# Banded attention with score tiles of 64 queries of two heads instead of 128 queries of one head

## The chip, the cores and the metric

The kernel runs on one core of a Trainium2 chip. The metric is the device time of one execution in microseconds (us). Three executions of the kernel before took 2079.76, 2080.51 and 2081.54 us, so the median is 2080.51 us. Five engines work side by side and meet through semaphores: PE (TensorE, matrix products into the PSUM banks), DVE (VectorE), ACT (ScalarE), POOL (GpSimd) and SP (it issues most of the transfers). PEld is the loading of PE's stationary operand.

## The reference

One encoder layer is applied to two sequences that share their weights, a sample of 1024 tokens and a prompt of 512, all in float32. Normalised tokens go through one input projection (2048 to 5632); half of the mix is a gated convolution branch, the other half is attention in a window; both are multiplied by a gate, joined, projected by `w_out`, added to the input and normalised. The part around the change is this:

```python
def banded_sink_attention(q, k, v, sink):        # 8 query heads, 2 key heads (GROUP = 4), head size 128
    ...                                          # query block b of 128 sees key blocks b-1, b, b+1
    s = jnp.einsum("bnqkgd,bnjkd->bnkgqj", qb, kb).astype(jnp.float32) * scale
    rel = kpos[:, None, :] - qpos[:, :, None]
    valid = (jnp.abs(rel) <= WINDOW) & (kpos[:, None, :] >= 0) & (kpos[:, None, :] < S)   # WINDOW = 128
    s = jnp.where(valid[None, :, None, None], s, -1e30)
    m = jnp.maximum(jnp.max(s, axis=-1, keepdims=True), sink_f)
    p = jnp.exp(s - m)
    denom = jnp.sum(p, axis=-1, keepdims=True) + jnp.exp(sink_f - m)
    probs = (p / denom).astype(v.dtype)
    o = jnp.einsum("bnkgqj,bnjkd->bnqkgd", probs, vb)
```

A query sees at most 257 keys: those at a distance of up to 128. All scores that are computed beyond that get the value -1e30 and come out of the exponential as zero.

## The kernel before

**Products.** Each float32 operand is split into a high part (rounded to the type float32r, by ACT) and a low part (the rest, by DVE); `parts` (L506) does this. A product is then three matmuls into one PSUM bank: high by high, high by low, low by high. The projections run as a written-out list of work items: `Unit` and `Onto` (L94, L271) multiply 2 by 2 blocks by Strassen's scheme with seven products, each of 12 matmuls with 512 columns (L207), and `Job` (L386) is a plain product of 512 columns (L670). PE works through this list for nearly the whole run.

**Lanes.** All else (convolution taps, normalisation, attention) is written as Python generators that sit in three lanes (`Lane`, L64). After every three matmuls of the list, `tick` gives each lane credit in ns, and a lane takes steps while it has credit; a `yield S1` says what the step is held to cost. So attention's matmuls are put between the matmuls of the projections. A scheduler then orders the instructions of each engine by priority (`high_priority`) and by when their operands come free.

**Attention.** `group` (L1116) holds keys and values of one key head and goes through the blocks of 128 queries: 8 blocks by 2 groups for the sample, in the trace from 876 to 1290 us, while the prompt's projections run on PE; 4 blocks by 2 groups for the prompt, from 1391 to 1670 us, while the sample's convolution output and then its output projection run. `attention` (L1151) does one block for the four heads of a group:

- the queries are split (L1160), and those of the next block are loaded (L1149, from `q_d` in device memory, where `rotated` and `rotate` stored them, L1073 to L1079);
- for each head, three matmuls (L1168) make a tile `s` of 128 queries by 384 keys (256 in the first and last block of a sequence); there are two PSUM buffers `s`;
- one DVE instruction (L1171) scales the tile, adds the mask, and writes it to a tile `p` together with the maximum of each row. `p` tiles come from a set of four buffers (`PT`, L487), which other parts of the program use too;
- ACT takes the exponential (L1182), with the row sums, and multiplies by the reciprocal (L1189);
- for each block of 128 keys, PE turns the four tiles (L1202, matmuls against the identity) into one PSUM tile `pt`, ACT and DVE split it into `a`, and three matmuls of 512 columns (L1197) add to `pv`;
- ACT copies `pv` out (L1210) and SP stores it in `att_d`.

**POOL** does nothing in the sample's attention. While the prompt's second group is under way, it issues the transfers of `Onto.begin` (L285): each loads a tile that a later product is added to, into a buffer `g` or `u`, and waits until that buffer's last user is done. Instructions of one engine run in order, so what stands behind such a transfer waits as well.

Of the kernel before, what the change touches and what calls it, by code (L numbers as in the profile page):

```python
# [25 lines left out]
LN_EPS = 1e-5  # L26
SCALE = P ** -0.5


# [401 lines left out]
class Encoder:  # L431
# [129 lines left out]
    def constants(self):  # L561
# [15 lines left out]
        def rest():  # L577
            self.ident = load("ident", [P])
            self.mask = load("mask", [3 * P])
# [166 lines left out]
class Sequence:  # L746


    def __init__(self, e, s):
# [322 lines left out]

    def rotated(self, dst, accs):  # L1073
        self.e.store(dst, self.rope(accs[0], 0))

    def rotate(self, dst):
        def done(t, z):
            self.e.store(dst[:, t * W : t * W + W], self.rope(z, t, z))
            yield  # L1079

        return done
# [26 lines left out]
    def query(self, h, accs):  # L1108
        self.rotated(self.q_d[h // GROUP][:, h % GROUP], accs)
        self.asked(h)  # L1110
# [35 lines left out]
    def load_query(self, g, b, room=None):  # L1146
        if b < self.B:
            self.q = room or self.e.U([GROUP, P])
            self.e.nc.sync.dma_start(self.q, self.q_d[g][:, :, b * P : (b + 1) * P])  # L1149

    def attention(self, g, b, k, v):  # L1151

        e, nc, B = self.e, self.e.nc, self.B
        lo, hi = max(b - 1, 0), min(b + 2, B)
        n = (hi - lo) * P
        keys = slice(lo * P, hi * P)
        mask = e.mask[:, (lo - b + 1) * P : (hi - b + 1) * P]
        qs = e.A([2, GROUP, P])
# [5 lines left out]
        pr = []  # L1164
        for h in range(GROUP):
            ps = e.PS("s", [3 * P])
            for p, (x, y) in enumerate(((0, 0), (0, 1), (1, 0))):
                nc.tensor.matmul(ps[:, 0:n], qs[:, x, h], k[y][:, keys], start=p == 0, stop=p == 2)  # L1168
            p = e.PT("p", NP, [W])
            with e.tc.high_priority(SOON):  # L1170
                nc.vector.tensor_tensor_reduce(  # L1171
                    p[:, 0:n], ps[:, 0:n], mask, SCALE, e.sink[:, g * GROUP + h : g * GROUP + h + 1],
                    ALU.add, ALU.max, accum_out=m[:, h : h + 1],
                )
            pr.append(p)
            if h % 2:
                yield S6
        with e.tc.high_priority(SOON):
            nc.vector.tensor_scalar(nm, m, -1.0, None, ALU.mult)  # L1179
            nc.vector.tensor_tensor(es, e.sink[:, g * GROUP : (g + 1) * GROUP], m, ALU.subtract)  # L1180
            for h, p in enumerate(pr):
                nc.scalar.activation(p[:, 0:n], p[:, 0:n], AF.Exp, bias=nm[:, h : h + 1], accum_out=l[:, h : h + 1])  # L1182
            nc.scalar.activation(es, es, AF.Exp)
        yield S2
        with e.tc.high_priority(SOON):
            nc.vector.tensor_tensor(l, l, es, ALU.add)
            nc.vector.reciprocal(r, l)
            for h, p in enumerate(pr):
                nc.scalar.activation(p[:, 0:n], p[:, 0:n], AF.Identity, scale=r[:, h : h + 1])  # L1189
        yield S4  # L1190
# [8 lines left out]
        for i in range(hi - lo):  # L1199
            tp = e.PS("pt", [GROUP, P])  # L1200
            for h, p in enumerate(pr):
                nc.tensor.transpose(tp[:, h], p[:, i * P : (i + 1) * P], e.ident)  # L1202
# [12 lines left out]
    def units(self):  # L1215
# [19 lines left out]
        rest = gates[:2] + [  # L1235
            both((K + g, V + g), f"kv{g}", each(self.rotate(self.k_d[g]), self.value_of(g))) for g in range(2)
        ]
        for h in range(HEADS):
            turn = self.rotate(self.q_d[h // GROUP][:, h % GROUP])
            rest.append(both((Q + h, AG + h), f"q{h}", each(turn, self.silu_of(self.ag_d[h]))))  # L1240
        return conv, rest + gates[2:]

    def jobs(self):
# [7 lines left out]
        kv = lambda g: [  # L1251
            job(K + g, lambda acc: self.rotated(self.k_d[g], acc)),
            job(V + g, lambda acc: self.value(g, acc)),
# [923 lines left out]
```

## Time and profile before

| what | value |
|---|---|
| median of three executions | 2080.51 us |
| span of the profiled execution, first to last instruction | 2072.4 us |
| profiled execution's own time | the page lists the span alone; the median lies 8.1 us above it |
| PE busy | 2057.6 us, 99% of the span |
| DVE busy | 1752.3 us, 85% |
| ACT busy | 1043.9 us, 50% |
| POOL busy | 157.8 us, 8% |
| DMA engines, share of 16 | q1 (SP) 61.6%, q0 (POOL) 12.1% |

"Busy" of PE counts from the start of a matmul to a modelled end, so 99% does not say how fast PE is within that time; the distance from one start to the next in the timeline does. The lines by group give the count and mean length of each kind of instruction; the list of waits says what an engine stood idle for.

### The profile page before, as it was taken

How to read it: one execution, taken by the hardware profiler on the slowest of the kernel's cores; microseconds unless marked ns; L12 is line 12 of the kernel's file. 1: busy time of each engine (PE TensorE's matmuls, PEld its weight loads, DVE VectorE, ACT ScalarE, POOL GpSimd, SP SyncE). 2: the span in 40 equal slices, each digit the busy share in tenths (PEclk: the TensorE clock that was granted, in tenths of full speed). 3: DMA queues.
4: the chain of work that ended last, by engine and by line, in shares of the span. 5: the costliest groups of instructions: out<-in, count | busy, mean ns of one | idle time of the engine just before them, and what ended most of it. 6: DMA issues, size and time to landing. Idle time of an engine off the chain costs nothing.

```text
span 2072.4 us, 27195 instructions
## 1 busy us (share of the span) xinstructions
PE 2057.6 (99%) x9256; PEld 1696.0 (82%) x9256; DVE 1752.3 (85%) x2873; ACT 1043.9 (50%) x1711; POOL 157.8 (8%) x240
## 2 busy tenths in 40 slices
PE   9999999999999999999999999999999999999998
PEld 8888888888888888788888888888888888888886
DVE  8767899998899999889866877767799978998877
ACT  7485445333464443644455777336454343454454
POOL 0111111101111112100000000000000111100000
PEclk9999999999999999999999999999999999999999
DMA  8888786864577776954455555997789899678897
GB/s 295 312 299 254 197 222 220 292 214 154 193 242 192 178 173 172 290 169 154 159 172 187 176 183 182 317 331 235 246 288 302 281 317 297 206 249 297 290 334 275
DMA packets 242300, 494.56 MB, mean 239 GB/s; under 512 B 23664, under 2 KB 84464, under 8 KB 242160
## 3 DMA queue, kind: packets, MB, share of 16 engines
q1 hardware_dynamic: 216352, 428.83, 61.6%
q0 software_dynamic: 24512, 61.88, 12.1%
q10 hardware_dynamic: 1296, 2.11, 0.3%
q8 instruction: 72, 1.18, 0.2%
q14 instruction: 68, 0.56, 0.1%
HBM read 331.77 MB, written 160.96 MB: 238 GB/s over the span
## 4 chain that ended last, share of the span: by engine, by line
PE 52%; issue 7%; DVE 4%; DMA 2%; POOL 1%; ACT 1%; POOLq 0%; ACTq 0%; SPq 0%; DVEq 0%
PE a L670 14%; PE c L670 7%; PE b L670 7%; PE a L207 7%; PE c L207 3%; PE s L1168 2%; PE pv L1197 2%; PE s L1851 2%; PE a L1851 2%; PE b L207 1%; PE pt L1202 1%; DVE hl L511 1%; PE pt L1851 1%; PE pv L1851 1%; POOL u L501 1%
## 5 line engine op out<-in xcount | busy, mean ns | idle before, releaser
L207 PE MATMUL a<-t,hl 128*128 128x512 f32 x2640 | 633.1, 390 | 2.0 <-ACT g L236 1.3
L207 PEld LDWEIGHTS a<-t,hl 128*128 128x128 f32 x2640 | 493.2, 188 | 109.5 <-ACT g L236 2.6
L510 ACT ACTIVATE hl<-raw 128x1024 fp32r<-128x1024 f32 (+3 forms) x334 | 296.1, 890 | 375.3 <-PE c L207 90.6
L511 DVE TENSOR_TENSOR hl<-raw,hl 128x1024 fp32r<-128x1024 f32 (+3 forms) x334 | 337.9, 1012 | 143.6 <-ACT hl L510 142.0
L670 PE MATMUL a<-t,hl 128*128 128x512 f32 x1344 | 325.8, 393 | 0.0
L207 PE MATMUL c<-t,hl 128*128 128x512 f32 x1320 | 319.2, 389 | 0.0
L670 PEld LDWEIGHTS a<-t,hl 128*128 128x128 f32 x1344 | 248.9, 188 | 50.2
L207 PEld LDWEIGHTS c<-t,hl 128*128 128x128 f32 x1320 | 247.4, 188 | 51.5 <-DVE u L304 0.2
L1041 DVE SCALAR_TENSOR_TENSOR f<-f,c_w_dw,f 128x512 f32<-128x512 f32 x248 | 173.3, 745 | 0.3
L670 PE MATMUL b<-t,hl 128*128 128x512 f32 x672 | 163.6, 393 | 1.3 <-DVE t L515 0.8
L1004 DVE SCALAR_TENSOR_TENSOR f<-f,c_w_dw,f 128x512 f32<-128x512 f32 x232 | 163.7, 745 | 1.0 <-ACT f L999 0.9
L670 PE MATMUL c<-t,hl 128*128 128x512 f32 x672 | 164.4, 393 | 0.0
L207 PE MATMUL b<-t,hl 128*128 128x512 f32 x660 | 159.8, 389 | 0.0
L670 PEld LDWEIGHTS b<-t,hl 128*128 128x128 f32 x672 | 124.6, 188 | 27.4 <-DVE t L515 1.1
L670 PEld LDWEIGHTS c<-t,hl 128*128 128x128 f32 x672 | 124.7, 188 | 24.7
L207 PEld LDWEIGHTS b<-t,hl 128*128 128x128 f32 x660 | 123.7, 188 | 25.6
L1033 DVE SCALAR_TENSOR_TENSOR f<-f,w_both,f 128x512 f32<-128x512 f32 x120 | 89.8, 748 | 2.3 <-ACT f L1027 0.3
L236 ACT ACTIVATE u<-a 128x512 f32<-128x512 f32 x82 | 48.7, 594 | 69.7 <-PE a L207 66.9
L236 ACT ACTIVATE g<-a 128x512 f32<-128x512 f32 x78 | 46.4, 595 | 70.0 <-PE a L207 65.1
L1182 ACT ACTIVATE p<-p,tiny 128x384 f32<-128x384 f32 (+1 forms) x96 | 54.5, 570 | 44.1 <-DVE tiny L1179 25.2
L510 ACT ACTIVATE a<-pt 128x512 fp32r<-128x512 f32 x64 | 38.0, 593 | 63.9 <-PE pt L1202 63.6
L418 ACT ACTIVATE hl<-raw 128x1024 fp32r<-128x1024 f32 x43 | 45.4, 1056 | 47.1 <-PE a L670 18.7
(354 smaller groups left out, 2713.0 us busy)
## 6 DMA issues: line engine op xcount, KB each, us to landing
raw<-w_in SPq DMA_DIRECT2D x170, 512.0 KB, 5.2
raw<-w_out SPq DMA_DIRECT2D x31, 512.0 KB, 5.3
raw<-w_pw SPq DMA_DIRECT2D x24, 512.0 KB, 4.2
wsum_P<-raw SPq DMA_DIRECT2D x47, 256.0 KB, 3.5
raw<-wsum_P SPq DMA_DIRECT2D x18, 512.0 KB, 4.7
f<-x_s SPq DMA_DIRECT2D x16, 512.0 KB, 8.7
g<-wsum_P SPq DMA_DIRECT2D x28, 256.0 KB, 4.4
a<-sum_S SPq DMA_DIRECT2D x24, 256.0 KB, 6.7
```

What stands on the lines that cost most here:

```text
L207: nc.tensor.matmul(acc, hl[:, l, o, j, :], toks[j][:, r], start=name in FRESH and j == 0 and q == 0, stop=name in LAST and j == HALF - 1 a ...
L236: nc.scalar.activation(t, bank, AF.Copy)
L418: e.nc.scalar.activation(t[:, 0], raw, AF.Copy)
L510: nc.scalar.activation(hi, x, AF.Copy)
L511: nc.vector.tensor_tensor(lo, x, hi.bitcast(F32), ALU.subtract)
L670: nc.tensor.matmul(job.acc[0], hl[:, l, kk // HALF, kk % HALF, :], r, start=i == 0 and p == 0, stop=i == nk - 1 and p == 2,)
L1004: nc.vector.scalar_tensor_tensor(t, h[:, j : j + T], w(j), t, ALU.mult, ALU.add)
L1033: nc.vector.scalar_tensor_tensor(m0, odd[:, j : j + H], both(j), m0, ALU.mult, ALU.add)
L1041: nc.vector.scalar_tensor_tensor(out, d[:, j : j + H], w(2 * j + k), out if j else m0, ALU.mult, ALU.add)
L1168: nc.tensor.matmul(ps[:, 0:n], qs[:, x, h], k[y][:, keys], start=p == 0, stop=p == 2)
L1182: nc.scalar.activation(p[:, 0:n], p[:, 0:n], AF.Exp, bias=nm[:, h : h + 1], accum_out=l[:, h : h + 1])
L1851: nc.tensor.matmul(acc[t], self.toks[name, m][:, x, i, t * P : (t + 1) * P], parts[i][l].rearrange("p a b -> p (a b)"), start=fresh and fi ...
```

## The change

A score tile now holds 64 queries of two heads: the first 64 rows are one head, the others the next head with the same 64 positions. Such a tile needs the keys from 128 before its first query to 128 after its last, 320 in place of 384; at the ends of a sequence 192 for the outer half and 256 for the inner. A block still has four tiles (two pairs of heads by two halves), with three matmuls each. The queries lie in device memory so that one load brings them in this order; to store them takes pieces of 64 values in place of 512. Mask and sinks are laid out to fit. The columns of `p` that no score is written to (64 of them in each tile that has fewer columns than its block has keys) are set to zero by GpSimd, since the turning of the tiles still takes blocks of 128 keys. Its output now goes to two heads by 64 queries of `pt`.

```diff
@@ Sequence
-        self.q_d = dram("q_d", [GROUP, self.T], 2)
+        self.q_d = dram("q_d", [GROUP // 2, self.T // HQ, 2, HQ], 2)
...
+    def rows_of_query(self, h):
+        pair, odd = divmod(h % GROUP, 2)
+        dst = self.q_d[h // GROUP][:, pair, :, odd, :]
+        n = W // HQ
+        return lambda t, z: self.e.store(dst[:, t * n : t * n + n], z.rearrange("p (n q) -> p n q", q=HQ))
...
     def load_query(self, g, b, room=None):
         if b < self.B:
             self.q = room or self.e.U([GROUP, P])
-            self.e.nc.sync.dma_start(self.q, self.q_d[g][:, :, b * P : (b + 1) * P])
+            src = self.q_d[g][:, :, 2 * b : 2 * b + 2].rearrange("p c a h q -> p c (a h q)")
+            self.e.nc.sync.dma_start(self.q.rearrange("p (c a) x -> p c (a x)", c=GROUP // 2), src)
 
     def attention(self, g, b, k, v):
...
-        n = (hi - lo) * P
-        keys = slice(lo * P, hi * P)
-        mask = e.mask[:, (lo - b + 1) * P : (hi - b + 1) * P]
+        tiles = []
+        for pair in range(GROUP // 2):
+            for half in range(2):
+                at = b * P + half * HQ
+                k0, k1 = max(at - P, 0), min(at + HQ + P, self.T)
+                tiles.append((slice(2 * pair, 2 * pair + 2), slice(half * HQ, half * HQ + HQ), k0, k1, k0 - at + P))
...
-        for h in range(GROUP):
+        for h, (heads, qr, k0, k1, at) in enumerate(tiles):
+            n = k1 - k0
             ps = e.PS("s", [3 * P])
             for p, (x, y) in enumerate(((0, 0), (0, 1), (1, 0))):
-                nc.tensor.matmul(ps[:, 0:n], qs[:, x, h], k[y][:, keys], start=p == 0, stop=p == 2)
+                nc.tensor.matmul(ps[:, 0:n], qs[:, x, h], k[y][:, k0:k1], start=p == 0, stop=p == 2)
             p = e.PT("p", NP, [W])
+            left, right = k0 - lo * P, hi * P - k1
+            if left:
+                nc.gpsimd.memset(p[:, 0:left], 0.0)
+            if right:
+                nc.gpsimd.memset(p[:, left + n : left + n + right], 0.0)
+            valid = p[:, left : left + n]
             with e.tc.high_priority(SOON):
                 nc.vector.tensor_tensor_reduce(
-                    p[:, 0:n], ps[:, 0:n], mask, SCALE, e.sink[:, g * GROUP + h : g * GROUP + h + 1],
+                    valid, ps[:, 0:n], e.mask[:, at : at + n], SCALE, e.sink[:, g * GROUP + h : g * GROUP + h + 1],
                     ALU.add, ALU.max, accum_out=m[:, h : h + 1],
                 )
...
-            for h, p in enumerate(pr):
-                nc.tensor.transpose(tp[:, h], p[:, i * P : (i + 1) * P], e.ident)
+            for (p, _), (heads, qr, *_) in zip(pr, tiles):
+                nc.tensor.matmul(
+                    tp[:, heads, qr], p[:, i * P : (i + 1) * P], e.ident.rearrange("p (h q) -> p h q", q=HQ),
+                    start=True, stop=True, is_transpose=True,
+                )
```

The exponential (L1182) and the multiplication (L1189) now work on `valid` as well. The order of the instructions shows three places.

On PE, in the sample's second block (the first with neighbours on both sides); `s` are score tiles, `t` the keys' parts, `a` the queries' parts, the others are the prompt's projections. Before:

```order
L1168 MATMUL s_7902<-t_966_7575,a_7866 128x384
L1168 MATMUL s_7902<-t_967_7576,a_7866 128x384
L1168 MATMUL s_7902<-t_966_7575,a_7866 128x384
L1168 MATMUL s_7908<-t_966_7575,a_7866 128x384
L1168 MATMUL s_7908<-t_967_7576,a_7866 128x384
L1168 MATMUL s_7908<-t_966_7575,a_7866 128x384
L670 MATMUL a_7879<-t_935_7399,hl_7810 128x512 x3
```

And now:

```order
L1183 MATMUL s_7904<-t_966_7575,a_7868 128x320
L1183 MATMUL s_7904<-t_967_7576,a_7868 128x320
L1183 MATMUL s_7904<-t_966_7575,a_7868 128x320
L1183 MATMUL s_7911<-t_966_7575,a_7868 128x320
L1183 MATMUL s_7911<-t_967_7576,a_7868 128x320
L1183 MATMUL s_7911<-t_966_7575,a_7868 128x320
L671 MATMUL a_7881<-t_935_7399,hl_7812 128x512 x3
```

The matmuls stand at the same place and are as many; each has 64 columns fewer.

On PE, the first turning of the same block's four tiles, with what each waits for. Before:

```order
L1202 MATMUL pt_8015<-c_ident,p_7906 128x128 [waits Activation_49]
L1202 MATMUL pt_8015<-c_ident,p_7912 128x128 [waits Activation_49]
L1202 MATMUL pt_8015<-c_ident,p_7924 128x128 [waits Activation_49]
L1202 MATMUL pt_8015<-c_ident,p_7930 128x128 [waits Activation_49]
```

And now:

```order
L1223 MATMUL pt_8021<-c_ident,p_7908 128x2x64 [waits Activation_49]
L1223 MATMUL pt_8021<-c_ident,p_7915 128x2x64 [waits Activation_49,Pool_49]
L1223 MATMUL pt_8021<-c_ident,p_7928 128x2x64 [waits Activation_49]
L1223 MATMUL pt_8021<-c_ident,p_7935 128x2x64 [waits Activation_49,Pool_49]
```

Tiles whose zeros stand in this block of keys make their matmul wait for POOL too. In the whole program, 20 of these matmuls waited for two engines before, and 64 do now.

On POOL and DVE, in the prompt's last block of the second group. POOL before:

```order
L285 DMA u_14576<-xT_s 128x512
L285 DMA g_14465<-xT_s 128x512
L285 DMA g_14549<-xT_s 128x512
L285 DMA g_14637<-xT_s 128x512
```

POOL now (`p_14498` and `p_14539` are the second and the fourth tile of the block):

```order
L286 DMA u_14656<-xT_s 128x512 [waits DMAHW3_49,DMAHW0_49,DMASW2_49]
L286 DMA g_14545<-xT_s 128x512 [waits DMAHW2_49,DMASW3_49]
L1187 MEMSET p_14498 128x64 [waits PE_49,Pool_49]
L286 DMA g_14629<-xT_s 128x512 [waits DMAHW3_49,DMAHW7_49,DMASW4_49,DVE_49]
L1187 MEMSET p_14539 128x64 [waits PE_49,Pool_49]
L286 DMA g_14717<-xT_s 128x512 [waits DMAHW0_49,DMASW5_49,DVE_49]
```

DVE now, around the fourth tile (`hl` are weights in two parts, `f` a convolution, L305 adds a finished product to its tile):

```order
L1192 ISA p_14539,tiny_14461<-s_14535,c_mask,c_attn_sink 128x192 [waits PE_49,Pool_49]
L1192 ISA tiny_14461 128x1
L1007 TENSOR_TENSOR f_13809<-f_13809 128x512 [waits DVE_49]
L1200 TENSOR_SCALAR tiny_14462<-tiny_14461 128x4 [waits DVE_49]
L1201 TENSOR_TENSOR tiny_14463<-c_attn_sink,tiny_14461 128x4
L305 TENSOR_TENSOR g_14449<-a_14339,g_14449 128x512 [waits DMAHW6_49,DMASW7_49,PE_49]
L512 TENSOR_TENSOR hl_14578<-raw_14376,hl_14578 128x1024 [waits Activation_49]
L305 TENSOR_TENSOR u_14475<-a_14547,u_14475 128x512 [waits DMAHW6_49,DMASW0_49,PE_49]
```

There are 80 memsets in all: 64 in the 16 blocks with neighbours on both sides, 16 in the 8 blocks at an end. 75 of the 96 DVE instructions of the score tiles wait for POOL, because the memset is the first to write the buffer and the others find out through it that the buffer is free; before, none did.

More of the change, by code (lines that the diff above doesn't have):

```diff
@@ L27 @@
 SCALE = P ** -0.5
+HQ = P // 2
 VAL, GLU, GATE, Q, K, V, AG = 0, 8, 16, 24, 32, 34, 36
@@ L1108, in query @@
     def query(self, h, accs):
-        self.rotated(self.q_d[h // GROUP][:, h % GROUP], accs)
+        self.rotated(self.rows_of_query(h), accs)
         self.asked(h)
@@ L1187, in attention @@
             nc.vector.reciprocal(r, l)
-            for h, p in enumerate(pr):
-                nc.scalar.activation(p[:, 0:n], p[:, 0:n], AF.Identity, scale=r[:, h : h + 1])
+            for h, (_, p) in enumerate(pr):
+                nc.scalar.activation(p, p, AF.Identity, scale=r[:, h : h + 1])
         yield S4
@@ L1235, in units @@
         rest = gates[:2] + [
-            both((K + g, V + g), f"kv{g}", each(self.rotate(self.k_d[g]), self.value_of(g))) for g in range(2)
+            both((K + g, V + g), f"kv{g}", each(self.rotate(self.rows_of(self.k_d[g])), self.value_of(g))) for g in range(2)
         ]
         for h in range(HEADS):
-            turn = self.rotate(self.q_d[h // GROUP][:, h % GROUP])
+            turn = self.rotate(self.rows_of_query(h))
             rest.append(both((Q + h, AG + h), f"q{h}", each(turn, self.silu_of(self.ag_d[h]))))
@@ L2154 @@
         arrays[name] = g[name].reshape(-1, P).T
-    arrays["attn_sink"] = np.broadcast_to(g["attn_sink"][0][None], (P, HEADS))
+    sink = g["attn_sink"][0].reshape(HEADS // 2, 2)[:, None, :, None]
+    arrays["attn_sink"] = np.broadcast_to(sink, (HEADS // 2, 2, 2, HQ)).transpose(2, 3, 0, 1).reshape(P, HEADS)
     half = P // 2
@@ L2162 @@
     arrays["sin"] = np.concatenate([sin, -sin])
-    q, k = np.arange(P)[:, None], np.arange(3 * P)[None] - P
+    q, k = np.arange(P)[:, None] % HQ, np.arange(2 * P + HQ)[None] - P
     arrays["mask"] = np.where(np.abs(k - q) <= P, f(0), f(-1e30)).astype(f)
```

20 lines of the change are left out of this document (11 added, 9 removed).

## The prediction

> **What bounds the kernel now.** I read the page's busy times first, then the windows of the two stretches with attention, then what PE waited for.
>
> ```profile
> span 2072.4 us, 27195 instructions
> PE 2057.6 (99%) x9256; PEld 1696.0 (82%) x9256; DVE 1752.3 (85%) x2873; ACT 1043.9 (50%) x1711; POOL 157.8 (8%) x240
> ```
>
> ```profile
> core 0: us, PE busy (x) PEld busy (x) DVE busy (x) ACT busy (x) POOL busy (x), PEclk, DMA share, GB/s
> 875.00:1280.00 405.00, 405.00 (x1916) 334.18 (x1915) 316.10 (x610) 236.00 (x419) 0.00 (x0) 1.00 0.53 170
> 1390.00:1670.00 280.00, 279.77 (x1299) 232.58 (x1299) 242.29 (x429) 137.00 (x251) 14.99 (x28) 1.00 0.81 268
> ```
>
> PE is busy for 405.00 of 405 us and 279.77 of 280 us there, at the full granted clock. DVE, with 78% and 87%, has room. The waits of PE (engine, line, releaser: us in total, times, longest; first and last of ten rows) say the same of the whole run:
>
> ```profile
> PE pt L559 <- DVE ones_r L574: 1.3, 1, 1.3
> ...
> PE a L207 <- DVE t L511: 0.2, 1, 0.2
> ```
>
> None of the ten is above 1.3 us. So PE's stream of matmuls sets the end, and PE time taken out of attention comes off the span, as long as nothing new makes PE wait.
>
> **Term 1, shorter score matmuls.** Their number and shapes, by form:
>
> ```profile
> L1168 PE MATMUL s<-t,a 128*128 128x384 f32 x144 | 29.5, 339 | 0.0
> L1168 PE MATMUL s<-f,a 128*128 128x384 f32 x48 | 9.8, 339 | 0.0
> L1168 PE MATMUL s<-f,a 128*128 128x256 f32 x48 | 7.2, 286 | 0.0
> L1168 PE MATMUL s<-t,a 128*128 128x256 f32 x48 | 7.2, 286 | 0.0
> ```
>
> 192 matmuls go from 384 to 320 columns; of the 96 with 256 columns, half (two tiles of four) go to 192 and half stay. The 339 and 286 ns are lengths of overlapping instructions; what one costs is the distance of starts. From PE's timeline (start us, length, instruction):
>
> ```profile
> 901.78 7.65 PE L670 MATMUL a<-t,hl 128*128 128x512 f32 x33
> 909.27 2.21 PE L670 MATMUL b<-t,hl 128*128 128x512 f32 x9
> ...
> 1028.22 1.22 PE L1168 MATMUL s<-t,a 128*128 128x384 f32 x6
> 1029.28 1.55 PE L670 MATMUL b<-t,hl 128*128 128x512 f32 x6
> ...
> 1054.31 0.89 PE L1168 MATMUL s<-t,a 128*128 128x256 f32 x6
> 1055.04 1.56 PE L670 MATMUL c<-t,hl 128*128 128x512 f32 x6
> ```
>
> Six with 384 columns take 1.06 us (177 ns each), six with 256 take 0.73 us (122), 33 with 512 take 7.49 us (227). So 64 columns are 25.0 ns between 384 and 512, 27.5 between 256 and 384, and 26.3 over the whole way, which I take: 192 x 26.3 = 5.05 us off. For 192 columns there is no row. By the same slope, 48 x 26.3 = 1.26 us off. The nearest rows are narrower matmuls of 128 columns, of two kinds:
>
> ```profile
> 1.32 3.89 PE L559 MATMUL pt<-ones_r 128*128 128x128 f32 x17 [1.32 <-DVE ones_r L574]
> 5.01 0.73 PE L349 MATMUL a<-t,hl 128*128 128x512 f32 x1
> ...
> 8.52 0.45 PE L559 MATMUL pt<-ones_r 128*128 128x128 f32 x3
> 8.81 0.68 PE L349 MATMUL a<-t,hl 128*128 128x512 f32 x2
> ```
>
> ```profile
> 911.31 0.60 PE L1202 MATMUL pt<-c_ident,p 128*128 128x128 f32 x4
> 911.67 2.33 PE L670 MATMUL b<-t,hl 128*128 128x512 f32 x9
> ...
> 963.31 0.60 PE L1202 MATMUL pt<-c_ident,p 128*128 128x128 f32 x4
> 963.67 2.33 PE L670 MATMUL a<-t,hl 128*128 128x512 f32 x9
> ```
>
> A turning matmul (L1202) costs 0.36 / 4 = 90 ns, a float32r one (L559) 97 ns at 8.5 us. Halfway between 90 at 128 columns and 122 at 256 is 106, so 192 columns save at least 16 ns: 48 x 16 = 0.8 us. From the other side, the first 17 of L559 took 217 ns each, 1.7 ns per column; at that rate 192 columns would cost 326 ns and lose 48 x 204 = 9.8 us. I take 1.26, since the rows at 8.5 us show the same instruction near a steady stream, and the start is the only place with the slow rate. Term 1 is **-6.3 us**, 5.6 to 6.6 without the slow case.
>
> **Term 2, turning.** As many matmuls of as many columns, whose output lies in two pieces of 64: no row shows that shape; I take zero, since the rate of L1202 and L559 differs by 7 ns only although operands and outputs differ. A loss has as its bound that all 256 cost as L559, 256 x 7 = 1.8 us; a gain I exclude, since no column goes. 44 more of them wait for two engines, which takes an instruction of its own in PE's queue:
>
> ```profile
> L1202 PEldq EVENT_SEMAPHORE  x20: 51/51/51, 959.2 to 1657.8; - x20
> ```
>
> If all showed, 44 x 51 ns = 2.2 us. I take zero: the one at 959.2 belongs to the group that PE starts at 963.31, so PE's queue had read 4 us ahead of the array, and that group took the same 0.36 us as the one at 911.31, which has none.
>
> **Term 3, the zeros.** 80 memsets on POOL. Nothing like 128x64 is in the trace, only four of 128x1:
>
> ```profile
> L2168 POOL MEMSET const-float32-0.0<- 128x1 f32 x1 | 0.1, 100 | 0.2 <-issue 0.2
> ```
>
> From 0.1 us up to the 0.55 us of a transfer's issue on POOL (below) bounds one; I take 0.2. POOL has nothing else to do in the sample's attention. A memset can run from the end of the block before (its last turning) to the next block's first score tile, and that tile's DVE instruction now waits for it. The shortest such gap:
>
> ```profile
> 1189.76 0.60 PE L1202 MATMUL pt<-c_ident,p 128*128 128x128 f32 x4
> 1192.04 0.52 PE L1168 MATMUL s<-t,a 128*128 128x384 f32 x2
> ```
>
> That is 2.3 us less 0.36, so two memsets of at most 0.55 fit. Cost zero, but for one place: in the prompt's last block, the fourth tile's memset stands behind a transfer that was issued late, and DVE's instruction for that tile behind the memset. POOL's timeline, then DVE's (the fourth tile; then the adding of a finished product):
>
> ```profile
> 1643.62 0.55 POOL L285 DMA_DIRECT2D g<-xT_s  x1
> 1650.63 0.55 POOL L285 DMA_DIRECT2D g<-xT_s  x1 [6.47 <-DMA wsum_P<-raw]
> ```
>
> ```profile
> 1647.96 0.48 DVE L1171 CUSTOM_DVE_ANT_0 p<-s,c_mask,c_attn_sink 128x256 f32<-128x256 f32 x1
> ...
> 1651.65 0.69 DVE L304 TENSOR_TENSOR u<-a,u 128x512 f32<-128x512 f32 x1
> ```
>
> ```profile
> 1650.97 2.88 PE L207 MATMUL b<-t,hl 128*128 128x512 f32 x12
> 1653.69 2.88 PE L207 MATMUL a<-t,hl 128*128 128x512 f32 x12
> ```
>
> DVE would stand until 1650.63 + 0.55 + 0.2 = 1651.4 in place of 1647.96, 3.4 us. Queued behind it are one add and the split of weights, then the add at 1651.65, which must end before PE overwrites bank `a` at 1653.69. It would come at about 1651.4 + 0.4 + 0.7 + 1.2 = 1653.7 and end 0.7 later: PE waits up to 0.7 us. I take +0.3; if the slack is gone altogether, 3.4.
>
> **Term 4, off the path.** DVE and ACT instructions get shorter (L1171 above took 0.48 us with 256 columns), all beside a busy PE: zero; it would count if DVE were the bound. The 24 stores of queries take pieces of 256 bytes in place of 2048:
>
> ```profile
> q1 hardware_dynamic: 216352, 428.83, 61.6%
> ```
>
> ```profile
> 680.00:860.00 180.00, 178.02 (x781) 145.32 (x780) 174.11 (x260) 82.26 (x130) 34.10 (x39) 1.00 0.75 192
> ```
>
> ```profile
> L504 SPq DMA_DIRECT2D att_d<-u x24: 524/561/571, 895.7 to 1669.8; - x24
> L504 SPq DMA_DIRECT2D q_d<-g x16: 319/320/320, 685.7 to 1025.5; - x16
> ```
>
> A packet takes 0.616 x 16 x 2072.4 us / 216352 = 94 ns of one DMA engine on average. A store has 128 packets of 2 KB now (0.75 us of all 16) and 1024 after. Bounds: the bytes alone, +0; 94 ns per packet, 6.0 us, +5.3. In 680 to 860 us, 16 such stores stand against 25% x 180 = 45 us of free time, so up to +2.8 each is absorbed. I take +1 to +2 each, hidden. Issuing on SP grows too (0.32 us for one piece per partition, 0.56 for four), by perhaps 0.6 x 24 us spread over 340; the loads of queries get fewer pieces. [...]
>
> **Sum.** 2072.4 - 6.3 + 0.3 = 2066.4 us of span. The median of the runs shown lies 8.1 us above the span, so **2074.5 us**, 0.29% less.
>
> **Rivals.**
> - *Part of it is eaten.* DVE's new wait for POOL costs PE at several blocks of the prompt's second group, where POOL issues transfers 28 times. Two full delays of 3.4 us, half of each reaching PE, give back 3.4: 2077.9. For: 75 of 96 score tiles now depend on POOL. Against: in the order, the memsets of that group's first three blocks stand behind transfers that the timeline shows issued well before those blocks' scores.
> - *Narrow matmuls are slow.* The 48 with 192 columns run at the rate of the first 17 of L559, +9.8 for -1.26: 2074.5 + 11.1 = 2085.6. Against: the 97 ns at 8.5 us.
> - *Slower, by the stores.* Place: 680 to 860 us, q1. At 94 ns per packet, 16 x 5.3 = 85 us of transfer meet 45 us free; the rest, up to 40 us, delays weights and PE: 2074.5 + 40 = 2114. It decides from +2.8 us per store, 55 ns per packet. For: POOL's transfers share these engines. Against: in the window no wait of PE is for a transfer, and a packet with an eighth of the bytes should not cost the full 94 ns.
> - *The gain is larger:* other rows of the order moved by a few places; 2071.
>
> **Chances.** Forecast (2073 to 2076) 0.60, eaten 0.20, narrow 0.05, stores 0.07, larger 0.08. What the runs can tell from no change is 0.2%, 4.2 us, so faster means under 2076.3. Faster: 0.60 + 0.08, less 0.02 at the edge, 0.66; same: 0.20 + 0.02, and 0.01 of a store case that is mostly absorbed, 0.23; slower: the rest, 0.11. The range leaves out the two slower rivals (0.12) and the far ends: 2071.0 to 2080.0; the forecast's own is 2073 to 2076.
>
> **What would show it.** Right: score groups of six at 0.91 us (320 columns) and 0.57 to 0.64 (192 by six); PE's waits no longer than now; turning at 0.36 us per four. Wrong: a wait of PE for DVE near 1650 us above 0.7 us or at each prompt block; waits for transfers before 1030 us; turning groups 50 ns or more longer; DVE waiting for POOL in the sample's blocks.

## The result and the profile after

The change makes the kernel **slower**: 2092.95 us against 2080.92 us (medians of six executions each, side by side on one chip), a ratio of 1.0053 with a 95% interval of 1.0040 to 1.0066. The prediction was 2074.5 us. 0.1% is 2.1 us throughout.

The page of the changed kernel (the profiled execution took 2097.32 us, the longest of the six):

```profile
span 2095.3 us, 27509 instructions
PE 2062.3 (98%) x9256; PEld 1693.4 (81%) x9256; DVE 1747.4 (83%) x2873; ACT 1033.8 (49%) x1711; POOL 168.2 (8%) x320
```

The span is 22.9 us longer than before's, more than the 12.0 us between the medians. The runs listed with their spans take about 2 us more than these, so the profiled execution of before took some 2074 us (an estimate), 6 to 7 below its median, and the change's took 4.4 above its own. What the two traces differ by is therefore in part the spread of executions. PE stands idle for 2095.3 - 2062.3 = 33.0 us, against 14.8 before: 18.2 us. It is also busy 4.7 us longer, although its matmuls have fewer columns. The windows of the two stretches with attention, and the stretch in which the sample's queries are stored (same columns as in the prediction):

```profile
875.00:1280.00 405.00, 401.31 (x1902) 327.70 (x1901) 312.22 (x608) 225.20 (x406) 6.99 (x54) 1.00 0.54 168
1390.00:1670.00 280.00, 269.36 (x1243) 221.94 (x1242) 234.81 (x417) 129.06 (x240) 16.82 (x48) 0.99 0.79 260
680.00:860.00 180.00, 178.00 (x780) 144.83 (x778) 175.12 (x262) 81.51 (x129) 33.37 (x39) 1.00 0.79 190
```

In the first two, PE is idle for 3.7 and 10.6 us, where it was idle for 0 and 0.2. In the third nothing has changed for PE (178.00, before 178.02), while the DMA share went from 0.75 to 0.79. What PE waited for (us in total, times, longest; the first four rows):

```profile
PE a L208 <- DVE tiny L1208: 5.5, 1, 5.5
PE a L671 <- ACT hl L511: 2.3, 1, 2.3
PE s L1183 <- DVE a L512: 2.3, 1, 2.3
PE a L1875 <- DVE f L1618: 1.9, 1, 1.9
```

Four single waits, none of them at a memset; before, the longest was 1.3 us. The clock granted to PE fell at three of them. Windows around these (same columns; the granted clock is the third figure from the end):

```profile
1060.00:1080.00 20.00, 17.17 (x71) 13.03 (x70) 10.56 (x17) 12.29 (x23) 0.30 (x2) 0.91 0.38 132
1590.00:1612.00 22.00, 16.50 (x67) 13.22 (x66) 14.34 (x25) 7.44 (x17) 2.75 (x5) 0.84 0.91 308
1925.00:1945.00 20.00, 18.14 (x77) 14.88 (x76) 14.74 (x28) 10.73 (x16) 0.00 (x0) 0.83 0.72 232
```

The clock records of this trace hold 1.0 and 0.5 only, so the means stand for 0.09 x 20 / 0.5 = 3.6, 0.16 x 22 / 0.5 = 7.0 and 0.17 x 20 / 0.5 = 6.8 us at half rate: 17.4 us. PE was at work in 12.6 us of these (the last section has the exact stretches), which cost half of that, 6.3 us. That is a part of the longer busy time: 2057.6 - 6.3 (term 1) + 6.3 = 2057.6, against 2062.3; where the other 4.7 us come from stays open.

What the prediction said of PE's own work came true. PE's timeline (start, length):

```profile
877.81 0.86 PE L1183 MATMUL s<-t,a 128*128 128x192 f32 x6
878.51 0.87 PE L671 MATMUL a<-t,hl 128*128 128x512 f32 x3
...
889.77 0.60 PE L1223 MATMUL pt<-c_ident,p 128*128 128x128 f32 x4
890.13 2.33 PE L671 MATMUL c<-t,hl 128*128 128x512 f32 x9
...
900.14 1.05 PE L1183 MATMUL s<-t,a 128*128 128x320 f32 x6
901.02 1.55 PE L671 MATMUL a<-t,hl 128*128 128x512 f32 x6
```

Six scores of 320 columns take 0.88 us (147 ns each, predicted 0.91 for six), three of 192 and three of 256 take 0.70 (so (0.70 - 3 x 0.122) / 3 = 111 ns for 192; the first row's x6 are three of each width), four turnings 0.36 as before. So the question is where the waits come from.

Two of them, read backwards. At 1068 us PE waits for the upper part of a weight (`hl`) that ACT makes:

```profile
1063.79 1.97 PE L671 MATMUL c<-t,hl 128*128 128x512 f32 x8
1068.07 0.73 PE L671 MATMUL a<-t,hl 128*128 128x512 f32 x2 [2.31 <-ACT hl L511]
```

```profile
1062.27 0.82 ACT L1000 ACTIVATE f<-f,c_b_dw,c_w_dw 128x512 f32<-128x512 f32 x1 [7.73 <-DMA f<-h_d]
1062.99 0.71 ACT L1001 ACTIVATE f<-f,c_w_dw 128x512 f32<-128x512 f32 x1
1063.71 1.28 ACT L1203 ACT_TABLE_LOAD   x1
...
1066.98 1.04 ACT L511 ACTIVATE hl<-raw 128x1024 fp32r<-128x1024 f32 x1
```

ACT stood for 7.73 us in front of the first instruction of a convolution, whose input (`h_d`) was still being loaded. Behind it in the queue stood the exponentials of an attention block and the weight that PE wanted. At 1601 us the chain goes over POOL:

```profile
1575.76 0.55 POOL L286 DMA_DIRECT2D g<-xT_s  x1 [1.81 <-DVE a L512]
1594.34 0.55 POOL L286 DMA_DIRECT2D g<-xT_s  x1 [18.03 <-DVE f L1350]
1594.89 1.16 POOL L286 DMA_DIRECT2D u<-xT_s  x2
```

```profile
1600.73 0.69 DVE L305 TENSOR_TENSOR u<-a,u 128x512 f32<-128x512 f32 x1 [3.35 <-DMA u<-xT_s]
```

```profile
1601.56 4.74 PE L208 MATMUL a<-t,hl 128*128 128x512 f32 x12 [5.50 <-DVE tiny L1208]
```

POOL stood 18.03 us for a buffer `g` that came free late, with two loads of `u` behind it. DVE waited 3.35 us for one of these, and PE 5.5 us for DVE (the releaser is named `tiny`, the instruction after the add; the add reads the bank `a` that PE is about to overwrite). The twelve matmuls behind took 4.74 us in place of 2.88, most of them at half rate.

The wait at 1931 us is of another kind: the DVE instruction that PE waited for (L1618) had itself waited for a load (`g<-gate_d`), and the traces of e4 to e7 below, which have the change's order there, show no such wait. So it is not put down to the order. The fourth, at 1548 us, comes up again below.

None of the late instructions read backwards here belongs to the change. What differs is their place in the queue. The order of the built program is another one from the sample's attention on: to get from one order to the other, at least 108 instructions have to be moved on PE, 164 on DVE, 28 on ACT, 3 on POOL and 74 on SP, the zeros not counted (counted in the fixed orders of e3 and e4 below).

### The profile page after: what moved, and what is told of

Its sections match the earlier page's. It is cut to its first block, busy times and chain, and to the rows that moved or that the text cites. A ratio compares the mean times of both kernels' runs of the same rounds, so it can differ in the third digit from the quotient of the medians.

```text
span 2095.3 us, 27509 instructions
## 1 busy us (share of the span) xinstructions
PE 2062.3 (98%) x9256; PEld 1693.4 (81%) x9256; DVE 1747.4 (83%) x2873; ACT 1033.8 (49%) x1711; POOL 168.2 (8%) x320
## 4 chain that ended last, share of the span: by engine, by line
PE 44%; issue 8%; DVE 7%; DMA 6%; ACT 1%; POOL 1%; SPq 0%; ACTq 0%; POOLq 0%; DVEq 0%
PE a L671 10%; PE a L208 6%; PE b L671 5%; PE c L671 5%; PE c L208 3%; PE a L1875 2%; PE pv L1218 2%; PE s L1875 2%; DMA a<-ag_d 2%; PE s L1183 2%; PE b L208 1%; PE pt L1223 1%; DVE hl L512 1%; DVE t L512 1%; PE pv L1875 1%
## 5 line engine op out<-in xcount | busy, mean ns | idle before, releaser
L1203 ACT ACTIVATE p<-p,tiny 128x320 f32<-128x320 f32 (+2 forms) x96 | 50.3, 525 | 37.2 <-DVE tiny L1201 28.7
```

The costliest lines, as they stand in the source:

```text
L1203: nc.scalar.activation(p, p, AF.Exp, bias=nm[:, h : h + 1], accum_out=l[:, h : h + 1])
```

## Experiments

Theory **order**: the loss comes from instructions that changed places in the engines' queues. An engine takes its queue in order, as ACT (7.73 us, waiting for a load) and POOL (18.03 us, waiting for a buffer) do in the traces above, so an instruction that waits for a transfer holds up what stands behind it. Rival **a part costs**: the zeros, the stores or the turning cost what the trace shows as waits.

**The parts alone, and the order alone.** Two kernels add one part to the kernel before. In both the scheduler leaves PE, DVE, ACT and POOL in the old order.

```diff
 e1, on the kernel before:
             p = e.PT("p", NP, [W])
+            if (h % 2 and b > 0) or (h % 2 == 0 and hi == b + 2):
+                x = 0 if h % 2 else n - P // 2
+                nc.gpsimd.memset(p[:, x : x + P // 2], 0.0)
 e2, on the changed kernel:
-                k0, k1 = max(at - P, 0), min(at + HQ + P, self.T)
+                k0, k1 = lo * P, hi * P
```

(e2's mask has 448 columns, and a tile of ones that is read in one column alone has only that one, to make room.) The other two fix the order. `ORDER` holds, for each engine, the places of its instructions in the order of the program text; it is taken from a built program, and a bare ordering edge, which waits for nothing, is drawn from each instruction to the next on its engine:

```diff
+def in_order(nc, tc):
+    traced = [i for i in nc.cur_bb.bb.instructions if not type(i).__name__.startswith("Bass")]
...
+    for code in ORDER.values():
...
+        own = [traced[k] for k in np.cumsum(steps)]
+        for before, i in zip(own, own[1:]):
+            tc.add_manual_dep(i, before.name, no_wait, reason="in_order")
     with tile.TileContext(nc) as tc, ExitStack() as ctx:
         encoder(ctx, tc, a)
+        in_order(nc, tc)
```

e3 is the changed kernel with the order of before; e4 is the kernel before with the order of the change.

> The kernel before, with the change's 80 memsets of 64 columns added on GpSimd (the score instruction on VectorE then overwrites them, so that it waits for GpSimd as in the change). Every engine's instructions keep the order they have before. Theory 'order' (the 12 us come from instructions that changed places in the engines' queues, which a waiting instruction then holds up): 2081 us, within 2 us of before, since no row changes places. Rival 'a part costs' in its first form, the zeros: VectorE waits for GpSimd, GpSimd's memsets stand behind its transfers, and PE waits: 2093 us or more (the change's loss of 12 us, and 6 us more that the shorter scores hide there, so up to 2099).

> The change's layout alone: tiles of 64 queries of two heads, queries stored in pieces of 256 bytes, turning into two pieces of 64, but all 384 (or 256) keys in every score matmul and a mask of 448 columns, so no zeros are needed. Every engine's order is that of before. Theory 'order': 2081 us, within 2 us of before. Rival 'a part costs', second form, the layout (stores in small pieces, turning): 2093 to 2099 us. My prediction's terms 2 and 4 stand here alone; it had 0 for both.

> The changed kernel, every instruction of it with its waits, but each engine issues its instructions in the order that the kernel before has (the zeros stand where they fall on GpSimd). Theory 'order': the prediction's terms stand without the new waits: 2080.9 - 6.3 = 2074.6 us, 2073 to 2077, and the half-rate stretches of the clock near 1070, 1600 and 1930 us are gone. Rival 'a part costs': what costs is in the instructions, not their places: 2090 to 2095 us as in the change. In between (2078 to 2088) both would have a share.

> The kernel before, no instruction changed, but each engine issues in the order that the changed kernel has (zeros left out). Theory 'order': the loss comes without the change: 2092.9 + 6.3 = 2099 us, 2094 to 2103, with PE waiting several us near 1060 and 1600 us. Rival 'a part costs': 2081 us, within 2 us of before.

Measured, with the kernel before at 2081.43 us beside them:

| run | median us | ratio to before, 95% interval |
|---|---|---|
| e1 zeros only | 2082.75 | 1.0005 (0.9996 to 1.0013) |
| e2 layout only | 2081.81 | 0.9998 (0.9989 to 1.0007) |
| e3 change, old order | **2073.30** | 0.9960 (0.9947 to 0.9972) |
| e4 before, new order | **2096.19** | 1.0075 (1.0062 to 1.0088) |

Zeros and layout, each alone, cost nothing that can be measured. The change in the old order is faster than before, by 8.3 us (5.8 to 11.0), and no kernel of this study is faster. The new order alone costs 15.6 us where no instruction is changed. Between the two orders of the changed kernel lie 1.0053 - 0.9960 = 0.93%, 19.4 us. e3's page and windows:

```profile
span 2070.0 us, 27512 instructions
PE 2052.4 (99%) x9256; PEld 1690.2 (82%) x9256; DVE 1747.9 (84%) x2873; ACT 1034.3 (50%) x1711; POOL 168.2 (8%) x320
```

```profile
875.00:1280.00 405.00, 404.48 (x1933) 333.11 (x1932) 315.15 (x614) 232.95 (x424) 6.99 (x54) 1.00 0.55 173
1390.00:1670.00 280.00, 278.18 (x1297) 230.79 (x1298) 241.70 (x430) 135.21 (x251) 18.86 (x51) 1.00 0.81 269
```

PE is idle for 0.5 and 1.8 us there. Theory order stands. No kernel was run with its own order fixed; that the ordering edges themselves cost nothing is argued from e3 and e4, which move in opposite directions. The next question is whether a few places make the 19 us, or many small ones.

**Two places put back.** In the listings, `-` marks a row at its place in the change's order and `+` the place that it is put back to.

```diff
 e5, ScalarE near 1067 us:
-ACTIVATE f<-f,c_b_dw,c_w_dw
-ACTIVATE f<-f,c_w_dw
...
 ACTIVATE hl<-raw
+ACTIVATE f<-f,c_b_dw,c_w_dw
+ACTIVATE f<-f,c_w_dw
 e6, GpSimd between 1575 and 1600 us:
-DMA g_13935<-xT_s
-DMA g_14039<-xT_s
 DMA u_13863<-xT_s
 DMA u_13956<-xT_s
+DMA g_13935<-xT_s
 DMA u_14070<-xT_s
+DMA g_14039<-xT_s
```

e7 has both, and the first two loads of the group in the old order (`g`, then `u`). e8 is the kernel before with the change's rows at the places of e5 and e6 alone.

> The changed kernel with its own order everywhere but at one place: on ScalarE, in the sample's attention, the two starting instructions of a convolution (which wait for the load of its input) stand behind the block's exponentials and the weights' upper part again, as before. Theory 'two places' (most of the loss is made where an instruction that waits for a transfer stands in front of others: here, and at GpSimd's five loads in the prompt's second group): the 2.3 us wait of PE near 1067 us and the half-rate stretch behind it go, 3.6 to 5 us: 2088 to 2090 us against 2093. Rival 'many small ones' (the loss is the sum of many displaced rows on VectorE and PE, each too small to see): 2092 us, under 2 us.

> The changed kernel with its own order everywhere but on GpSimd, where five loads of partial products (u, u, g, u, g) in the prompt's second group stand as before, so that the one that waits longest for its buffer is last but one again and not second. Theory 'two places': the 5.5 us wait of PE near 1600 us and the half-rate stretch behind it go, 4.7 to 7.4 us: 2086 to 2088 us. Rival 'many small ones': 2092 us.

> Both of the former together, and the swap of GpSimd's first two loads of that group undone too: ten displaced rows out of some 360. Theory 'two places': 8 to 13 us come back: 2080 to 2085 us. Rival 'many small ones': 2091 us.

> The kernel before, its instructions and order, but with these two places as the change has them: on ScalarE the convolution's start ahead of the exponentials, on GpSimd the five loads in the change's order. Theory 'two places': 8 to 12 us are lost without the change: 2089 to 2093 us. Rival 'many small ones': 2082 us, within 2 us of before.

Before was 2080.46 us here. e5: 2086.23 us, 1.0024 (1.0013 to 1.0035), so against the change's 1.0053 6.0 us come back, more than expected. e6: 2088.66, 1.0041 (1.0029 to 1.0053), 2.5 us, half of what I expected. e7: 2083.41, 1.0011 (1.0002 to 1.0020), 8.7 us, the low end of 8 to 13. e8: 2086.55, 1.0029 (1.0019 to 1.0040), 6.0 us lost, below the 8 to 12. A difference of two such ratios is known to about 3 us either way, so e6's 2.5 us alone is not clear of noise. The two places together make nearly half of the loss (8.7 of 19.4 us), and some 10 us are still open. e3's ACT at the first place, where the convolution's input is there by the time that its turn comes:

```profile
1062.00 1.04 ACT L514 ACTIVATE hl<-raw 128x1024 fp32r<-128x1024 f32 x1
1062.95 0.80 ACT L1003 ACTIVATE f<-f,c_b_dw,c_w_dw 128x512 f32<-128x512 f32 x1
```

and e3's POOL at the second, where the two loads of `u` go first and none waits for 18 us:

```profile
1569.42 0.55 POOL L289 DMA_DIRECT2D u<-xT_s  x1 [9.71 <-DVE a L515]
1573.41 0.55 POOL L289 DMA_DIRECT2D u<-xT_s  x1 [3.45 <-DMA att_d<-u]
1574.03 0.55 POOL L289 DMA_DIRECT2D g<-xT_s  x1
```

**Where the rest is.** The start of the same matmul of PE's list in two traces gives a lag. Lag against e3 at six times of e3's trace (us; e9 to e18 follow):

| kernel | 1000 | 1067 | 1482 | 1544 | 1608 | 1782 |
|---|---|---|---|---|---|---|
| change | 1.1 | 6.2 | 6.1 | 9.8 | 18.5 | 20.3 |
| e7 | 1.4 | 1.6 | 2.2 | 6.6 | 12.9 | 13.8 |
| e9 sample new | 3.5 | 8.1 | 7.6 | 8.3 | 8.2 | 10.1 |
| e13 | -0.3 | -0.1 | -1.2 | -1.1 | -0.8 | 1.0 |
| e12 prompt new | 1.2 | 1.3 | 10.8 | 14.7 | 23.1 | 22.9 |
| e10 | -1.9 | -1.8 | -2.1 | 1.6 | 6.4 | 6.1 |
| e11 | 2.4 | 2.6 | 2.1 | 5.2 | 6.1 | 6.7 |
| e14 | 1.7 | 2.0 | 2.9 | 7.1 | 7.2 | 7.4 |
| e15 | -0.9 | -0.8 | -1.4 | 4.8 | 3.6 | 3.8 |
| e16 | -0.2 | 0.1 | 0.7 | 6.7 | 6.2 | 8.4 |
| e17 | 2.5 | 2.7 | 2.1 | 2.7 | 3.9 | 6.7 |
| e18 | 0.9 | 1.1 | 0.1 | 4.3 | 5.6 | 7.8 |

The change's lag grows at three places: up to 1067, 1482 to 1544, and 1544 to 1608. (Behind 1782 it grows to 25.0 by the wait at 1931.) Lags of a few us that build up slowly are not read: each row is one execution, and not always one near its median. The traces of e3 and e13 are of the fastest execution of each, that of e17 is of the longest of nine. e9 and e12 cut the program in two: e9 is the changed kernel with the change's order up to about 1300 us and the old one behind, e12 the reverse. e10 is e7 with a third place put back, e11 is e10 with all engines in the old order from about 1560 us on.

```diff
 e10, ScalarE near 1520 us:
-ACTIVATE t_1910<-f_1894
 ACTIVATE u_1884<-pv_1871
-ACTIVATE t_1911<-f_1894
 ACTIVATE f_1885<-a_1887
+ACTIVATE t_1910<-f_1894
+ACTIVATE t_1911<-f_1894
-ACTIVATE hl_1909<-raw_1883
 ACTIVATE t_1912<-f_1895
+ACTIVATE hl_1909<-raw_1883
```

> The changed kernel; up to about 1300 us (the sample's attention) each engine issues in the change's order, from there on in that of before. Theory 'places' (the loss sits at a few places where an in-order queue stands; the one in the sample is ScalarE's at 1067 us): against the changed kernel in the old order (2073.3) only that place is left, 5 to 6 us: 2079 us, 2077 to 2081. Rival 'many small ones' (displaced rows everywhere, in proportion): the sample has 57 of PE's 61 displaced stretches and more than half of VectorE's, so at least half of the 19 us: 2083 us or more.

> The complement: the order of before up to about 1300 us, the change's from there on. Theory 'places': the waits near 1545, 1600 and behind stay, 10 to 13 us: 2084 to 2087 us. Rival 'many small ones': 2080 us or less. With the former run the two losses should add up to that of the whole order, 19 us; if not, the places feed each other.

> The kernel with ten displaced rows put back (2083.4), and six rows of ScalarE more: near 1520 us, where upper parts of sums that wait for loads stand ahead of the copy of an attention product and of a key's upper part in the change's order. Theory 'places': VectorE no longer stands 2 to 3 us for ScalarE near 1530, the 2.8 us wait of PE near 1550 goes with its half-rate stretch, 4.3 us: 2079 us. Rival 'many small ones': 2083 us; VectorE's own rows there (sums ahead of the queries' split) hold it up as before.

> As the former, and from about 1560 us on all engines in the order of before (there ScalarE's start of the prompt's convolution stands ahead of weight parts and exponentials in the change's order, and 145 rows of VectorE have moved with it). Theory 'places': the last 5 us between 1585 and 1621 go as well: 2074 to 2077 us. Rival 'many small ones' (300 displaced rows are still as in the change): 2079 us or more.

Before was 2081.93 us. e9: 2081.93, 0.9997 (0.9989 to 1.0006), 7.7 us above e3, between the two expectations. e12: 2096.02, 1.0059 (1.0047 to 1.0071), 20.6 us above e3, far over the 10 to 13. The losses add up to 28 us, not 19. The table shows why: e12 already lags by 10.8 us at 1482, although the change loses nothing between 1067 and 1482 (6.2 and 6.1). Behind the seam between the two orders it has two stalls that the change does not have, of 3.61 us at 1347 and 2.72 us at 1401, each with slower matmuls behind it: 46 took 12.38 us where the next 48 took 11.04, and 9 took 3.38 us where 12 took 2.89 at 1405.95. In the first DVE waits 4.93 us for ACT and PE for DVE:

```profile
1346.74 12.38 PE L674 MATMUL b<-t,hl 128*128 128x512 f32 x46 [3.61 <-DVE hl L515]
```

```profile
1354.81 1.23 DVE L515 TENSOR_TENSOR hl<-raw,hl 128x1024 fp32r<-128x1024 f32 x1 [4.93 <-ACT hl L514]
```

From 1482 on e12 loses 22.9 - 10.8 = 12.1 us, as theory places had it, and the change 14.2. e10: 2084.72, 1.0014 (1.0006 to 1.0022): nothing came back, a miss. The lag still grows by 3.7 us between 1482 and 1544 (4.4 in e7); only the waits changed. e11: 2080.03, 0.9989 (0.9980 to 0.9998): 5.2 us less than e10, and the growth from 1544 to 1608 went from 4.8 to 0.9 us, as expected; 2080 is above the expected 2077; the lag of 3.1 us between 1482 and 1544 is still there.

**One place among hundreds, and the third place.** e13 is e9 with ACT's two instructions near 1067 us put back as in e5. e14 to e16 are e11 with SP's, DVE's, or both engines' rows between 1480 and 1560 us put back.

> The kernel with the change's order up to about 1300 us and the old one behind (2081.9), and on ScalarE near 1067 us the convolution's two starting instructions put back behind the exponentials; all other rows of the sample's attention stay as the change has them. Theory 'places': the 7 us of that half go with this one place: 2075 us, 2073 to 2077. Rival 'many small ones': 2080 us or more.

> The kernel with the first to the fourth place put back (2080.0), and SyncE's loads and stores between about 1480 and 1560 us in the old order (there three loads of sums had moved ahead of a load of weights). Theory 'the lag of 1483 to 1549 is SyncE's: ScalarE waits for loads that now come in another order': 2076 to 2077 us. Rival 'it is VectorE's order': 2080 us.

> As the run before, but instead of SyncE's rows VectorE's rows between about 1520 and 1560 us are put back (query and key splits and score instructions ahead of splits of sums again). Theory 'SyncE': 2080 us. Rival 'VectorE': 2076 to 2077 us, with PE's wait for the query's split near 1545 us gone.

> Both put back. If either theory is right, 2076 to 2077 us; if neither, 2080 us and the cause lies before 1480 us. If only both together bring it, each run alone stays at 2080.

Before was 2081.29 us. e13: 2075.22, 0.9973 (0.9963 to 0.9983), as theory places expected: two instructions of ACT make 5.0 of e9's 7.7 us, and in e13's trace the rows that stay displaced in the sample make no lag (the 2.7 us between the medians of e13 and e3 are within the noise of 3). PE's longest waits in e9 and in e13:

```profile
PE a L211 <- DVE u L308: 2.2, 2, 1.6
PE a L674 <- ACT hl L514: 2.2, 1, 2.2
```

```profile
PE a L211 <- ACT g L240: 1.3, 2, 1.1
PE pt L563 <- DVE ones_r L578: 1.3, 1, 1.3
```

e14: 2078.41, 0.9987 (0.9979 to 0.9996). e15: 2079.63, 0.9989 (0.9981 to 0.9998). e16: 2079.01, 0.9986 (0.9976 to 0.9996). All three are as e11: neither SP nor DVE nor both. In e16 the trace still has PE waiting near 1545 us for a late DVE, and DVE for a weight part of ACT:

```profile
1542.30 1.23 DVE L515 TENSOR_TENSOR hl<-raw,hl 128x1024 fp32r<-128x1024 f32 x1 [1.84 <-ACT hl L514]
1543.44 0.69 DVE L515 TENSOR_TENSOR f<-a,f 128x512 fp32r<-128x512 f32 x1
1544.04 0.68 DVE L308 TENSOR_TENSOR u<-a,u 128x512 f32<-128x512 f32 x1
```

```profile
1544.87 4.18 PE L211 MATMUL a<-t,hl 128*128 128x512 f32 x9 [2.93 <-DVE u L308]
```

On ACT that weight part stands behind a part of a sum (`t`) in the change's order. e17 is e16 with these three rows back, e18 is e11 with them back:

```diff
 ScalarE near 1540 us:
-ACTIVATE t_1926<-f_1905
+ACTIVATE hl_1934<-raw_1899
 ACTIVATE f_1886<-a_1888
-ACTIVATE hl_1934<-raw_1899
+ACTIVATE t_1926<-f_1905
```

> The kernel with VectorE's and SyncE's rows between 1480 and 1560 us put back (2079.0), and three rows of ScalarE near 1540 us as well (weight part, key part, then the sum's part). Theory 'the lag is ScalarE standing for a sum in front of a weight part': the 4 to 6 us go, 2074 to 2076 us. Rival 'its cause lies before 1480 us': 2079 us.

> The same three rows of ScalarE put back, but VectorE's and SyncE's rows left as the change has them between 1480 and 1560 us (2080.0 without the three rows). Theory 'ScalarE alone': 2075 to 2077 us. Rival 'three queues together' (VectorE's splits of sums and SyncE's loads hold it up as well): 2079 to 2080 us, while the run before is at 2075.

e17: 2076.15 (before 2081.29), 0.9973 (0.9963 to 0.9983), 2.7 us below e16. e18: 2079.50, 0.9989 (0.9980 to 0.9998), as e11. The medians alone show this only just; the lags from 1482 to 1544 show it more plainly: they grow by 3.1 us in e11, 4.2 in e14, 6.2 in e15, 6.0 in e16 and 4.2 in e18, and by 0.6 in e17. So ACT's rows bring their gain only where rows of DVE and SP are back too (with one of the two alone they were not tried), and the cause does not lie before 1480 us, as my expectation for e16 had it. In e17 the weight part is made at 1537.80 and PE waits 0.53 us:

```profile
1537.80 1.05 ACT L514 ACTIVATE hl<-raw 128x1024 fp32r<-128x1024 f32 x1
```

```profile
1543.25 2.33 PE L211 MATMUL a<-t,hl 128*128 128x512 f32 x9 [0.53 <-DVE u L308]
```

(The execution of this trace lost its time later, behind 1608.) Put together in ratios: the place at 1067 us 6.0 us (e5), POOL's loads 2.7 (e7 against e5), ACT's rows near 1520 us -0.6 (e10 against e7), the stretch from 1560 us on 5.2 (e11 against e10), the place at 1540 us 3.3 (e17 against e11): 16.6 of the 19.4 us. Each of these is known to 2.5 to 3.5 us either way, so the 6.0, the 5.2 and the 3.3 are clear of zero and the other two are not. The last 2.7 us, between e17 and e3, are not clear of zero either, and stay open.

## Why the prediction was wrong

The table of lags and the runs name one failed step, the last of term 4; the others held.

- **Term 1, the shorter scores: right, and the exact sum by luck.** 177 - 147 = 30 ns for 320 columns and 122 - 111 = 11 ns for 192 give 192 x 30 + 48 x 11 = 6.3 us, the predicted sum with another split. I had 26.3 ns for both, and "at least 16" for 192 columns: one was too low by 0.7 us in all, the other too high by 0.7. In the old order the change brings 8.3 us (5.8 to 11.0), and the forecast's -6.0 lies inside.
- **Term 2, the turning, and the event instructions: right.** 0.36 us per four, and e2 has no cost.
- **Term 3, the zeros: right in total, with the place of its 0.3 us wrong.** A memset takes 0.15 us, and e1 is at 1.0005 (0.9996 to 1.0013). No wait of DVE is put down to GpSimd in the trace, and PE does not wait in the prompt's last block, where I had put 0.3 us.

```profile
L1189 POOL MEMSET p<- x40: 151/152/488, 852.9 to 1616.6; 128x64 f32 x40
```

- **Term 4, the stores: right that they stay hidden.** A store of queries lands after 3.4 us in the change and 3.1 before (KB each, median us to landing):

```profile
q_d<-g SPq DMA_DIRECT2D x16, 256.0 KB, 3.4
```

```profile
q_d<-g SPq DMA_DIRECT2D x16, 256.0 KB, 3.1
```

The DMA share in 680 to 860 us rose by 0.04, 7.2 us over 16 stores, 0.45 us each, less than the 1 to 2 that I took (the shares are rounded to 0.01, so 0.45 is good to 0.1), and e2 shows that the run time doesn't feel it.

- **Term 4, "DVE and ACT instructions get shorter ... zero": this step failed.** It priced the instructions and not their order. The scheduler orders each queue by when it holds operands to come free, so shorter score tiles gave the queues another order, and that cost 19.4 us, three times term 1. That it is the sizes follows from e1 and e2: with the memsets alone, or the layout with all the keys, the scheduler leaves PE, DVE, ACT and POOL in the old order. I had said that DVE has room, 22% and 13% of its time. A mean says nothing of one instruction that waits 7.73 us at the head of a queue with PE's next weight behind it. My condition "as long as nothing new makes PE wait" was checked at the memsets and the stores alone. The order was there to read: two instructions that wait for a load had moved ahead of the exponentials on ACT, and two loads of `g` ahead of two of `u` on POOL.
- **The rivals.** I had moved rows in the list only as a gain ("other rows of the order moved by a few places; 2071"), with 0.08; moved rows were the main effect, with the other sign. "Part is eaten" had the right stretch (the prompt's second group, POOL's queue) and the wrong culprit, the memsets. "Slower by the stores" and "narrow matmuls" fall with e2 and with the 111 ns. The 8.1 us that the sum adds to the span are no fixed cost: they are some 2 us and the distance of a short profiled execution from its median.
- **The signs.** Four signs said right or wrong as they should: 0.88 us for 0.91, 0.36 for the turning, no wait of PE put down to a transfer, and PE's waits much longer than before, which is the one that told. One missed: six matmuls of 192 columns take 6 x 111 = 0.67 us, just above my 0.57 to 0.64.

## What to carry to other kernels

When a scheduler orders the queues, a change of sizes is also a change of order: compare the order on every engine, and for each row that moved ahead ask what it waits for and what now stands behind it. To tell a change from its reordering, fix the order and run both ways; here this showed a gain of 8 us under a loss of 19. Putting rows back one queue at a time can show nothing where several queues hold each other, and a seam between two orders can make a stall of its own.

## What the runs showed of the hardware

A gap of PE can be paid twice. In the trace of the change, the stretches at half rate ahead of the last 6 us are these (same columns):

```profile
1069.46:1072.87 3.41, 3.41 (x9) 2.67 (x10) 3.41 (x7) 3.02 (x6) 0.00 (x0) 0.50 0.62 171
1598.52:1605.35 6.83, 3.79 (x9) 3.04 (x10) 3.97 (x7) 2.44 (x5) 0.52 (x1) 0.50 1.00 368
1929.62:1936.45 6.83, 5.43 (x13) 4.32 (x14) 5.14 (x11) 3.28 (x5) 0.00 (x0) 0.50 0.98 352
```

The first begins 1.4 us after an idle time of 2.31 us that ended at 1068.07, and right behind a further one of 0.53 us. The second begins inside the idle time of 5.50 us that ended at 1601.56, the third inside the one of 1.85 us that ended at 1931.02. PE works for 3.41 + 3.79 + 5.43 = 12.6 us of them, and loses 6.3 us on top of the gaps: the 9 matmuls at 1069.33 took 3.92 us, where 9 at 1609.33 took 2.22, and the 12 at 1601.56 took 4.74 in place of 2.88. The kernel before and e3 have no wait above 1.5 us and a mean clock of 0.999; in the kernel before it is 1.00 up to 2066 us and 0.56 from there on, where PE has no work left. A gap does not always do it. In the change itself the wait of 2.29 us at 1548 is followed by no stretch at half rate (1.00 from 1072.87 to 1598.52), although the one of 1.85 us at 1931 goes with one. In e8, PE's longest wait and the window around it are

```profile
PE a L673 <- ACT hl L513: 1.9, 1, 1.9
```

```profile
1060.00:1080.00 20.00, 17.53 (x81) 13.29 (x80) 11.92 (x23) 12.75 (x24) 0.00 (x0) 1.00 0.50 170
```

at full rate throughout. In e17, PE's longest wait is 1.8 us, and the trace has a mean clock of 0.997: 0.003 x 2079.1 / 0.5 = 12.5 us at half rate (an estimate, good to 2 us), where the 0.999 of e3 stands for 4.1 in the same way. What decides was not tried; with it, the price of a gap differs by up to 2.7 us (half of 5.43, an estimate).
